# Zero-padded keys for the second attention score product, and mLSTM state products issued by head pairs

## The chip, the cores and the metric

The kernel runs on one core of one Trainium2 chip. The metric is the device time of one execution in microseconds (us); lower is better. Five engines work side by side, each through its own queue in order: TensorE (PE: matmuls and transposes, with its weight loads shown apart as PEld), VectorE (DVE), ScalarE (ACT), GpSimd (POOL) and SyncE (SP, which here only issues DMAs).

## What is computed

A trunk of two encoder layers is applied to 768 tokens of width 1024: a sample of 256 tokens and a prompt of 512, which share the weights but not the attention. All of it is in fp32. Cut to the mixer, in which the change lies, the reference is:

```python
def block(args):                       # differential attention, 4 heads, 2 components of 64 each
    s = jnp.einsum('bqhcd,bshcd->bhcqs', qi, k)
    p = jax.nn.softmax(s + bias[None, :, None], axis=-1)
    a = p[:, :, 0] - lam * p[:, :, 1]
    return jnp.einsum('bhqs,bshd->bqhd', a, v)
...
# bidirectional mLSTM, 4 heads, chunks of 128 positions; C_prev is the state at the chunk's border
sqk = jnp.einsum('bhcjd,bhcsd->bhcjs', qf, kc) * P
num = (e_inter[..., None] * jnp.einsum('bhcjd,bhcde->bhcje', qf, C_prev)
       + jnp.einsum('bhcjs,bhcse->bhcje', sqk, vc))
den = e_inter * jnp.einsum('bhcjd,bhcd->bhcj', qf, n_prev) + jnp.sum(sqk, -1)
h = num / jnp.maximum(jnp.abs(den), jnp.exp(-m_out))[..., None]
```

Both are joined, projected, normalised, and followed by a conv-gated feed-forward part with a second normalisation.

## The kernel before

Each layer runs in stages: gates and input projections of the mLSTM; four attention heads (`att_in(h)` projects a head's queries and keys, `att(h)` computes it), woven with the mLSTM and with projections that are needed later; the output projection with the first normalisation; the feed-forward part. In the profiled execution the attention heads and the mLSTM outputs stand at about 110 to 356 us (layer 0) and 1040 to 1292 us (layer 1).

Precision is kept by splitting fp32 numbers into two fp32r parts and taking three products. For the attention scores the two parts of the queries (64 rows each) are stacked over the 128 rows of the array: `sQ[:, c]` holds high and low part of component c's queries, `sK[:, c]` the high part of its keys twice. One product over 128 rows (line 701) so gives two of the three terms. The third, high query times the keys' low part `kL`, is a product over 64 rows (line 702): rows 0 to 63 for component 0, rows 64 to 127 for component 1. There are 96 of these pairs (2 layers, 4 heads, 6 query tiles, 2 components), 64 with 512 keys and 32 with 256. They write the two banks of PSUM with tag "s"; DVE reduces them (line 703), ACT exponentiates (707), DVE combines the components (708 to 710), PE transposes (713), ACT or DVE copies (715), PE multiplies with the values (717), ACT squares (719).

For the mLSTM outputs of a chunk (`lstm_out`), each head adds, for each direction, a state product over 64 rows (line 611; heads 0 and 2 lie on rows 0 to 63, heads 1 and 3 on rows 64 to 127) and an own-key product over 128 rows (612). Heads take the banks "L" and "t" in turn. DVE and ACT then empty the bank (614 to 619), ACT squares into a scratch tile `jk` (621). The decay factors `pt` of a chunk come by DMA into one of two buffers (568) and get a mask on DVE (570) and eight exponentials on ACT (572).

Products over 64 rows are also the scores of the mLSTM (596), and the state updates (551) use 64 columns of the array at a time. All other products use the whole array.

A scheduler fixes the order of each engine's queue when the kernel is built. `weave` mixes the generators in proportion to their steps, and `prio` shifts their priority; waiting is left to semaphores. An instruction that waits holds up all that stands behind it on its engine.

```python
PE.matmul(ps[:, :n], sQ[:, c, qtok], sK[:, c, keys], start=True, stop=False)
PE.matmul(ps[:, :n], sQ[r, c, qtok], kL[r, keys], start=False, stop=True)
```

Of the kernel before, what the change touches and what calls it, by code (L numbers as in the profile page):

```python
# [13 lines left out]
F32 = mybir.dt.float32  # L14
F32R = mybir.dt.float32r
AF = mybir.ActivationFunctionType
ALU = mybir.AluOpType
# [12 lines left out]
# tokens are held as [sample 256 | prompt 512]  # L30
# [65 lines left out]
class Weights:  # L96
    """Weight blocks of up to 528 columns in the order of their use, each split into two fp32r parts.
    A block is a piece of DRAM, or a difference of two earlier ones (a dict, for Strassen's products)."""

    def __init__(self, nc, raw_pool, hl_pool, prio):  # L100
        self.nc, self.raw_pool, self.hl_pool, self.prio = nc, raw_pool, hl_pool, prio
        self.dram, self.blocks = [], []     # DRAM pieces; (source, n, destination or None)
        self.uses, self.raw, self.hl = {}, {}, {}
        self.n_dma = self.n_conv = self.n_got = self.n_done = 0
        self.diff_pool = None
        self.urgency = PR_CONV

# [17 lines left out]
    def _pieces(self, src):  # L125
        """DRAM pieces that the conversion of a block reads"""
        if not isinstance(src, dict):
            return [src]
        if src.get("planned"):
            return []  # L130
        src["planned"] = True
        return self._pieces(src["a"]) + self._pieces(src["b"])

# [1 line left out]
    def _load(self):  # L135
        # slots are reused in turn
# [40 lines left out]
    def pump(self):  # L177
        # activations (with a destination of their own) take no slot
# [27 lines left out]
def trunk(ctx, nc, tc, d, o, depth=DEPTH):  # L206
# [13 lines left out]
    def prio(offset):  # L220
        """instructions that the scheduler takes as if written that many earlier (or later)"""
# [9 lines left out]
    def lam_products(v):  # L231
        # lam = exp(q1.k1) - exp(q2.k2) + lam_init, held negated
        v = v.rearrange("p (l a b) -> p l a b", l=DEPTH, a=4)
        V.tensor_tensor(out=lprod, in0=v[:, :, 0::2, :], in1=v[:, :, 1::2, :], op=ALU.mult)

# [9 lines left out]
    # two token tiles at once while the first weights arrive  # L245
# [19 lines left out]
    for l in range(depth):  # L265
# [19 lines left out]
        for kind, i in ffn_seq:  # L285
            if kind == "f":
                # Strassen-Winograd: B = [[g0, u0], [g1, u1]], halves of the rows of w_gate and w_up
# [26 lines left out]
    lprod = sm.tile([128, DEPTH, 2, 64], F32, tag="lprod", name="lprod", bufs=1)  # L314
# [11 lines left out]
    def late_constants():  # L326
        nc.scalar.dma_start(attg, d["attg"])
        nc.scalar.dma_start(convw, d["conv"])
        V.reduce_sum(lsum, lprod, axis=X)
# [12 lines left out]
    def tok_major(t, blocks, ps, cols):  # L342
        """ps[tok, :] = sum over k of x[tok, k] W[k, cols]"""
# [4 lines left out]
    def feat_major(blocks, psA, psB):  # L348
        """ps[feature, tok] = sum over k of W[k, feature] x[tok, k]"""
# [9 lines left out]
    def transposed_split(src, name, tag, hi, lo):  # L359
        """src [128, 512] -> four transposed 128x128 blocks, split into hi and lo [128, 4, 128]"""  # L360
# [7 lines left out]
    # =====================================================================================  # L368
    for l in range(depth):
        RA = ExitStack()  # L370
        ra = RA.enter_context(tc.tile_pool(name=f"ra{l}", bufs=1, reuse_waits="tile", side="right"))
        hq = ra.tile([128, NT, 512], F32, name="hq")         # mLSTM q | k, then h in their place
        av = ra.tile([128, NT, 512], F32, name="av")         # attention values, then the heads' transposed outputs
        sQ = ra.tile([128, 2, T], F32R, name="sQ")
        sK = ra.tile([128, 2, T], F32R, name="sK")
        kL = ra.tile([128, T], F32R, name="kL")
# [5 lines left out]
        cols = lp.tile([128, NT, 3, 8], F32, name="cols")   # w, exp(-m_out), e_end  # L382
# [10 lines left out]
        G.tensor_scalar(lstmg, lstmg, 0.5 * math.sqrt(128.0), 0.0, op0=ALU.mult, op1=ALU.add)   # rsl lacks the root  # L393
# [32 lines left out]
        def gates():  # L426
            GP = ExitStack()
            gp = GP.enter_context(tc.tile_pool(name=f"gp{l}", bufs=1, reuse_waits="tile"))
            rmask = gp.tile([128, 384], F32, name="rmask")
# [4 lines left out]
            for di in range(2):  # L434
                for pr in range(2):
                    for hh in range(2):
# [6 lines left out]
            V.tensor_scalar(g1, f, 0.0, 1.0, op0=ALU.min, op1=ALU.mult)               # min(f, 0)  # L443
            V.tensor_scalar(g2, f, 0.0, 1.0, op0=ALU.max, op1=ALU.mult)
            V.tensor_tensor(out=g1, in0=g1, in1=g2, op=ALU.subtract)                  # -|f|
            S.activation(g1, g1, AF.Exp)                                              # e
            V.tensor_scalar(g2, g1, 1.0, 1.0, op0=ALU.add, op1=ALU.mult)              # u = 1 + e
# [5 lines left out]
                                   in1=g1.rearrange("p a b c -> p (a b c)"), op0=ALU.add, op1=ALU.subtract)   # (u - 1) - e  # L453
            V.reciprocal(g2, g2)
            V.tensor_tensor(out=g1, in0=g1, in1=g2, op=ALU.mult)
            V.tensor_tensor(out=g3, in0=g3, in1=g1, op=ALU.subtract)                  # log1p(e)
# [7 lines left out]
            t1 = gp.tile([128, T], F32, name="t1")  # L464
# [22 lines left out]
            # stabiliser at the start of each chunk, in scan order  # L487
# [8 lines left out]
            V.tensor_tensor(out=mr, in0=mo, in1=bc, op=ALU.subtract)                  # M  # L496
# [4 lines left out]
            V.tensor_tensor(out=t1[0:64, :], in0=ig, in1=bc, op=ALU.subtract)         # w  # L501
# [83 lines left out]
        def lstm_out(lc, c):  # L585
# [5 lines left out]
            # heads on different rows of the array write different banks  # L591
# [11 lines left out]
            yield  # L603
            for h in range(4):
                pr, r = h // 2, slice((h % 2) * 64, (h % 2) * 64 + 64)
                pn = P(TAG_NUM[h], f"num{c}{h}")
                for di in range(2):
                    w = pn[:, di * 256:di * 256 + 129]
                    first = di not in dirs
                    if not first:  # L610
                        PE.matmul(w, qet[r, di, pr, :], cst[di, c][r, pr, :], start=True, stop=False)
                    PE.matmul(w, pt[:, di, h, :], vaug[:, c, h, :], start=first, stop=True)
# [7 lines left out]
                jk = lc.tile([128, 128], F32, tag="jk", name=f"jk{c}{h}", bufs=2)  # L620
                S.activation(jk, hs, AF.Square, accum_out=ssq[:, c, h:h + 1])
# [19 lines left out]
        def ev_lo(t, p):  # L641
# [6 lines left out]
            # 2 sigmoid(x) = exp(min(x, 0)) (1 + tanh(|x| / 2)), exact for either sign; the gain holds the half  # L648
# [9 lines left out]
        def att_in(h):  # L658
# [4 lines left out]
            for ui, uu in ((0, uq), (1, uk)):  # L663
# [4 lines left out]
                for ps, tk in ((pBu, slice(0, SB)), (pA, slice(SB, T))):  # L668
# [5 lines left out]
                    else:  # L674
# [4 lines left out]
                        V.tensor_tensor(out=kL[lo_, tk], in0=ps[lo_], in1=sK[lo_, 0, tk].bitcast(F32), op=ALU.subtract)  # L679
                        V.tensor_tensor(out=kL[hi_, tk], in0=ps[hi_], in1=sK[hi_, 1, tk].bitcast(F32), op=ALU.subtract)  # L680
                yield

# [1 line left out]
        def att(h):  # L684
            slope = 2.0 ** (-8.0 * (h + 1) / 4)
            for s0, s1 in SEQ_ORDER[h]:
# [6 lines left out]
                for qt in range(nq):  # L693
# [4 lines left out]
                    for c in range(2):  # L698
                        ps = P("s", f"s{h}{s0}{qt}{c}")
                        r = slice(c * 64, (c + 1) * 64)  # L700
                        PE.matmul(ps[:, :n], sQ[:, c, qtok], sK[:, c, keys], start=True, stop=False)
                        PE.matmul(ps[:, :n], sQ[r, c, qtok], kL[r, keys], start=False, stop=True)
                        V.tensor_tensor_reduce(out=tp[:, c, :n], in0=ps[:, :n], in1=dneg[:, 384 - 128 * qt:384 - 128 * qt + n], scale=-slope, scalar=3e38,
                                               op0=ALU.add, op1=ALU.min, accum_out=mn[:, c:c + 1])
                    # tp holds -scores: exp(min - tp) = exp(scores - max)
# [12 lines left out]
                    jk = ra.tile([128, 128], F32, tag="jk", name=f"jka{h}{s0}{qt}", bufs=1)  # L718
# [373 lines left out]
```

## Time and profile before

| | |
|---|---|
| device time, median of 3 runs | 1888.2 us (1887.25 to 1888.33) |
| span of the profiled execution (first to last instruction) | 1882.1 us |
| PE busy | 1838.9 us (98%) |
| DVE busy | 1342.5 us (71%) |
| ACT busy | 771.7 us (41%) |
| POOL busy | 238.8 us (13%) |
| granted TensorE clock, mean | 0.996 |

The page gives the profiled execution by its span alone, 6.1 us under the median of the runs. Busy shares are averages over stages with different limits. A PE that counts as busy is not one that works at its best rate: the profile's matmuls overlap in the pipeline, so what one of them costs is read from the time between its start and the next one's start, not from its own duration.

### The profile page before, as it was taken

How to read it: one execution, taken by the hardware profiler on the slowest of the kernel's cores; microseconds unless marked ns; L12 is line 12 of the kernel's file. 1: busy time of each engine (PE TensorE's matmuls, PEld its weight loads, DVE VectorE, ACT ScalarE, POOL GpSimd, SP SyncE). 2: the span in 40 equal slices, each digit the busy share in tenths (PEclk: the TensorE clock that was granted, in tenths of full speed). 3: DMA queues.
4: the chain of work that ended last, by engine and by line, in shares of the span. 5: the costliest groups of instructions: out<-in, count | busy, mean ns of one | idle time of the engine just before them, and what ended most of it. 6: DMA issues, size and time to landing. Idle time of an engine off the chain costs nothing. (4 is left out here: it accounts for less than half of the span.)

```text
span 1882.1 us, 26221 instructions
## 1 busy us (share of the span) xinstructions
PE 1838.9 (98%) x9692; PEld 1592.7 (85%) x9692; DVE 1342.5 (71%) x2576; ACT 771.7 (41%) x1624; POOL 238.8 (13%) x256
## 2 busy tenths in 40 slices
PE   8899999999999999999998999999999999999998
PEld 8777777779899899899897777777898998998996
DVE  5445776489886786787954457765898877877878
ACT  4344565334443343343332445654253432433330
POOL 1000101042110111110110011010411111111102
PEclk9999999999999999999999999999999999999999
DMA  6212110311222121122233021104022221221221
GB/s 196 85 49 68 46 45 23 135 40 62 85 81 66 59 82 62 64 77 87 100 107 90 18 68 51 40 23 150 25 68 96 68 79 62 71 76 57 79 62 67
DMA packets 83279, 134.94 MB, mean 72 GB/s; under 512 B 7984, under 2 KB 27056, under 8 KB 83152
## 3 DMA queue, kind: packets, MB, share of 16 engines
q1 hardware_dynamic: 82432, 132.90, 22.0%
q8 instruction: 76, 1.25, 0.3%
q14 instruction: 51, 0.42, 0.1%
q10 hardware_dynamic: 720, 0.37, 0.1%
HBM read 126.86 MB, written 6.39 MB: 71 GB/s over the span
## 5 line engine op out<-in xcount | busy, mean ns | idle before, releaser
L915 PE MATMUL p<-actA,wh 128*128 128x384 f32 x1408 | 363.4, 338 | 3.2 <-DVE g L940 3.2
L171 ACT ACTIVATE wh<-raw 128x512 fp32r<-128x512 f32 (+1 forms) x348 | 215.7, 629 | 299.8 <-PE p L915 109.7
L172 DVE TENSOR_TENSOR wl<-raw,wh 128x512 fp32r<-128x512 f32 (+1 forms) x348 | 242.7, 707 | 95.9 <-ACT wh L171 95.4
L915 PE MATMUL p<-actB,wh 128*128 128x384 f32 x1056 | 270.1, 337 | 0.0
L915 PEld LDWEIGHTS p<-actA,wh 128*128 128x128 f32 x1408 | 254.7, 188 | 5.8 <-DVE g L940 3.8
L915 PE MATMUL p<-actA,wl 128*128 128x384 f32 x704 | 237.3, 337 | 0.0
L149 POOL TENSOR_TENSOR T<-raw,raw 128x512 f32<-128x512 f32 x88 | 120.7, 1374 | 836.5 <-DVE wl L172 483.6
L975 PE MATMUL dn<-wh,actB 128*128 128x512 f32 x576 | 208.7, 396 | 1.1 <-DVE acc L982 1.1
L171 ACT ACTIVATE wh<-T 128x512 fp32r<-128x512 f32 x176 | 108.3, 628 | 220.2 <-DVE acc L982 105.0
L915 PEld LDWEIGHTS p<-actB,wh 128*128 128x128 f32 x1056 | 191.2, 188 | 0.0
L975 PE MATMUL dn<-wh,ring 128*128 128x512 f32 x480 | 179.2, 397 | 1.8 <-DVE acc L982 1.8
L915 PE MATMUL p<-actB,wl 128*128 128x384 f32 x528 | 177.2, 336 | 0.0
L982 DVE TENSOR_TENSOR acc<-acc,dn 128x512 f32<-128x512 f32 x144 | 98.1, 681 | 72.0 <-PE dn L975 71.8
L172 DVE TENSOR_TENSOR wl<-T,wh 128x512 fp32r<-128x512 f32 x176 | 129.6, 748 | 22.1 <-ACT wh L171 21.9
L975 PEld LDWEIGHTS dn<-wh,actB 128*128 128x128 f32 x576 | 108.0, 188 | 28.7 <-DVE acc L982 2.8
L915 PEld LDWEIGHTS p<-actA,wl 128*128 128x128 f32 x704 | 132.2, 188 | 0.1
L871 PE MATMUL wo<-wh,actB 128*128 128x512 f32 x384 | 122.7, 396 | 0.0
L975 PE MATMUL dn<-wl,actB 128*128 128x512 f32 x288 | 113.2, 393 | 0.0
L975 PEld LDWEIGHTS dn<-wh,ring 128*128 128x128 f32 x480 | 90.0, 188 | 24.8 <-DVE acc L982 4.4
L915 PEld LDWEIGHTS p<-actB,wl 128*128 128x128 f32 x528 | 99.1, 188 | 0.0
L356 PE MATMUL aqkA<-actA,wh 128*128 128x512 f32 x256 | 97.7, 407 | 0.0
L975 PE MATMUL dn<-wl,ring 128*128 128x512 f32 x240 | 94.6, 394 | 0.0
(263 smaller groups left out, 3442.8 us busy)
## 6 DMA issues: line engine op xcount, KB each, us to landing
raw<-in_w_g_dram SPq DMA_DIRECT2D x88, 256.0 KB, 2.7
raw<-in_w_u_dram SPq DMA_DIRECT2D x88, 256.0 KB, 2.7
raw<-in_w_down_dram SPq DMA_DIRECT2D x88, 256.0 KB, 2.9
raw<-in_w_out_dram SPq DMA_DIRECT2D x32, 256.0 KB, 2.6
pt<-scr_m SPq DMA_DIRECT2D x12, 512.0 KB, 5.9
raw<-in_w_c_dram SPq DMA_DIRECT2D x16, 264.0 KB, 3.9
raw<-in_w_av_dram SPq DMA_DIRECT2D x16, 256.0 KB, 4.8
raw<-in_w_aq_dram SPq DMA_DIRECT2D x16, 256.0 KB, 3.5
```

What stands on the lines that cost most here:

```text
L149: src["engine"].tensor_tensor(out=src["tile"], in0=a, in1=b, op=ALU.subtract)
L171: self.nc.scalar.activation(h, v, AF.Identity)
L172: self.nc.vector.tensor_tensor(out=l, in0=v, in1=h.bitcast(F32), op=ALU.subtract)
L356: PE.matmul(psA, w, actA[:, k, b, SB:T], start=n == 0, stop=n == 23)
L871: PE.matmul(p, actB[:, k, a, t * 128:(t + 1) * 128], units[k][1 + b], start=n + i == 0, stop=n == 7 and i == 2)
L915: PE.matmul(ps, blk[1 + a][:, k * 128:(k + 1) * 128], x[:, k, b, :], start=k + i == 0, stop=k == 3 and i == 2)
L975: PE.matmul(p, x, (wh_, wl_)[b], start=k + i == 0, stop=k == nf - 1 and i == 2)
L982: V.tensor_tensor(out=z, in0=z, in1=p, op=ALU.add)
```

## The change

- `kL` becomes two planes of 128 rows. Plane 0 holds component 0's low keys on rows 0 to 63 and zeros below, plane 1 component 1's on rows 64 to 127 and zeros above. The zeros are written by two memsets on POOL once per layer. The second score product then runs over all 128 rows, with the same stationary operand as the first.
- The state products of a pair of heads, of all their directions, are issued first, then the own-key products of both heads. Both banks of the pair are asked for together.
- To make room, the squares go where a dead value lies: the mLSTM's into `pt` instead of `jk`, the attention's into `aT` instead of another `jk`; the gates' mask shares the tile `t1`; the lambda products are formed in place, and their sum is taken at once.

```diff
-        kL = ra.tile([128, T], F32R, name="kL")
+        kL = ra.tile([128, 2, T], F32R, name="kL")
+        G.memset(kL[64:128, 0].bitcast(F32), 0.0)
+        G.memset(kL[0:64, 1].bitcast(F32), 0.0)
...
-                        V.tensor_tensor(out=kL[lo_, tk], in0=ps[lo_], in1=sK[lo_, 0, tk].bitcast(F32), op=ALU.subtract)
-                        V.tensor_tensor(out=kL[hi_, tk], in0=ps[hi_], in1=sK[hi_, 1, tk].bitcast(F32), op=ALU.subtract)
+                        V.tensor_tensor(out=kL[lo_, 0, tk], in0=ps[lo_], in1=sK[lo_, 0, tk].bitcast(F32), op=ALU.subtract)
+                        V.tensor_tensor(out=kL[hi_, 1, tk], in0=ps[hi_], in1=sK[hi_, 1, tk].bitcast(F32), op=ALU.subtract)
...
-                        PE.matmul(ps[:, :n], sQ[r, c, qtok], kL[r, keys], start=False, stop=True)
+                        PE.matmul(ps[:, :n], sQ[:, c, qtok], kL[:, c, keys], start=False, stop=True)
...
+            pns = {}
             for h in range(4):
-                pr, r = h // 2, slice((h % 2) * 64, (h % 2) * 64 + 64)
-                pn = P(TAG_NUM[h], f"num{c}{h}")
-                for di in range(2):
-                    w = pn[:, di * 256:di * 256 + 129]
-                    first = di not in dirs
-                    if not first:
-                        PE.matmul(w, qet[r, di, pr, :], cst[di, c][r, pr, :], start=True, stop=False)
-                    PE.matmul(w, pt[:, di, h, :], vaug[:, c, h, :], start=first, stop=True)
+                if h % 2 == 0:
+                    pair = [(hh, P(TAG_NUM[hh], f"num{c}{hh}")) for hh in (h, h + 1)]
+                    for di in dirs:
+                        for hh, pn in pair:
+                            r = slice((hh % 2) * 64, (hh % 2) * 64 + 64)
+                            PE.matmul(pn[:, di * 256:di * 256 + 129], qet[r, di, hh // 2, :], cst[di, c][r, hh // 2, :],
+                                      start=di == dirs[0], stop=False, skip_group_check=True)
+                    for hh, pn in pair:
+                        for di in range(2):
+                            PE.matmul(pn[:, di * 256:di * 256 + 129], pt[:, di, hh, :], vaug[:, c, hh, :],
+                                      start=not dirs and di == 0, stop=di == 1, skip_group_check=True)
+                    pns.update(pair)
+                pn = pns.pop(h)
...
-                jk = lc.tile([128, 128], F32, tag="jk", name=f"jk{c}{h}", bufs=2)
-                S.activation(jk, hs, AF.Square, accum_out=ssq[:, c, h:h + 1])
+                S.activation(pt[:, 0, h, :], hs, AF.Square, accum_out=ssq[:, c, h:h + 1])
...
-                    jk = ra.tile([128, 128], F32, tag="jk", name=f"jka{h}{s0}{qt}", bufs=1)
-                    S.activation(jk, pu[:, qt * 128:(qt + 1) * 128], AF.Square, accum_out=ssu[:, qt:qt + 1])
+                    S.activation(aT[:, 0:128], pu[:, qt * 128:(qt + 1) * 128], AF.Square, accum_out=ssu[:, qt:qt + 1])
```

In the built order of PE, a run is an unbroken stretch of products that use a part of the array (64 rows, or 64 columns), between products that use all of it. The change alters their number:

| runs, by the product that opens them | before | changed |
|---|---|---|
| second score product (L702; L709 in the changed kernel) | 96 | 0 |
| mLSTM state products (L611; L614) | 62 | 44 |
| mLSTM scores (L596; L598) | 20 | 24 |
| state updates (L551; L553) | 12 | 16 |
| one small product of the gates (L515; L517) | 2 | 2 |
| all | 192 | 86 |

PE, chunk 3 of layer 0, heads 2 and 3: `num` is a head's bank, `cst` the state and `vaug`, `pt` the operands of the own-key product, `lo` a projection. Before:

```order
L611 MATMUL num_2476<-cst_1670,qet_2117 128x129
L612 MATMUL num_2476<-vaug,pt_2105 128x129
L611 MATMUL num_2476<-cst_1751,qet_2117 128x129
L612 MATMUL num_2476<-vaug,pt_2105 128x129
L730 MATMUL aoT_2546<-ident,ao_2544 128x128 x2
L346 MATMUL lo_2723<-wh_1561,actA 128x512
L346 MATMUL lo_2723<-wl_1562,actA 128x512
L611 MATMUL num_2489<-cst_1670,qet_2117 128x129
L612 MATMUL num_2489<-vaug,pt_2105 128x129
L611 MATMUL num_2489<-cst_1751,qet_2117 128x129
L612 MATMUL num_2489<-vaug,pt_2105 128x129
```

The same place on PE in the changed kernel, with a head's second score product (L709) now a product of 128 rows:

```order
L709 MATMUL s_2661<-kL,sQ 128x512
L614 MATMUL num_2448<-cst_1664,qet_2097 128x129
L614 MATMUL num_2448<-cst_1743,qet_2097 128x129
L618 MATMUL num_2448<-vaug,pt_2085 128x129 x2
L736 MATMUL aoT_2516<-ident,ao_2514 128x128 x2
L345 MATMUL lo_2686<-wl_1634,actA 128x512
L708 MATMUL s_2665<-sK,sQ 128x512
L614 MATMUL num_2449<-cst_1664,qet_2097 128x129
L614 MATMUL num_2449<-cst_1743,qet_2097 128x129
L618 MATMUL num_2449<-vaug,pt_2085 128x129 x2
L709 MATMUL s_2665<-kL,sQ 128x512
```

Each head's two directions now stand side by side, one run in place of two, but the scheduler has kept the two heads of the pair apart.

DVE, the mask of chunk 4's decay factors in layer 0 (`pt` with `tri`), among the chunk before's work: `kq` are the mLSTM scores, `sg` the output gate, `tp` and `mn` the attention's reduction. Before:

```order
L598 TENSOR_TENSOR pt_2105<-kq_2416,pt_2105 128x4x128
L628 SCALAR_TENSOR_TENSOR hq<-hq,rsl,lstmg 128x128 x4
L570 TENSOR_TENSOR pt_2394<-pt_2394,tri 128x512 x2
L598 TENSOR_TENSOR pt_2105<-kq_2420,pt_2105 128x4x128
L715 COPY aT_2444<-aT_2441 128x256
L654 SCALAR_TENSOR_TENSOR sg_2527<-sgt_2528,sg_2527 128x512
L722 SCALAR_TENSOR_TENSOR sm_2368<-sm_2368 128x2
L703 ISA tp_2553,mn_2554<-s_2556,dneg 128x512
```

The same place on DVE in the changed kernel:

```order
L710 ISA tp_2523,mn_2524<-s_2526,dneg 128x512
L710 ISA mn_2524 128x1
L636 SCALAR_TENSOR_TENSOR hq<-hq,rsl,lstmg 128x128 x4
L600 TENSOR_TENSOR pt_2085<-kq_2391,pt_2085 128x4x128
L717 SCALAR_TENSOR_TENSOR tp_2400<-tp_2400,cc_2402 128x256
L662 SCALAR_TENSOR_TENSOR sg_2497<-sgt_2498,sg_2497 128x512
L600 TENSOR_TENSOR pt_2085<-kq_2395,pt_2085 128x4x128
L572 TENSOR_TENSOR pt_2369<-pt_2369,tri 128x512 x2
L722 COPY aT_2419<-aT_2416 128x256
```

The mask (now L572) stands behind the second score multiplication, the gate and an attention reduction that it stood ahead of. In the feed-forward parts no engine's order differs; at the start of layer 0 some projections of the first two token tiles change places on PE, and POOL has the two memsets among its first constants.

## Rows read from the trace of the kernel before

**Rows 1.** The page's first part: busy us, share of the span, instructions.

```profile
PE 1838.9 (98%) x9692; PEld 1592.7 (85%) x9692; DVE 1342.5 (71%) x2576; ACT 771.7 (41%) x1624; POOL 238.8 (13%) x256
```

**Rows 2.** Windows by stage: stretch, its length, busy us (count) by engine, clock, DMA.

```profile
110.00:160.00 50.00, 49.86 (x228) 36.42 (x226) 23.49 (x63) 21.86 (x58) 0.83 (x2) 1.00 0.06 18
236.00:310.00 74.00, 73.73 (x390) 54.98 (x388) 50.56 (x167) 45.20 (x142) 8.50 (x12) 1.00 0.13 36
```

**Rows 3.** Waits of PE in the whole span: us, times, longest.

```profile
PE s L701 <- ACT sK L677: 1.2, 2, 0.6
```

**Rows 4.** Timeline of PE, layer 0, head 1: start us, us, line, tiles.

```profile
202.34 0.50 PE L701 MATMUL s<-sK,sQ 128*128 128x512 f32 x1
202.77 0.50 PE L702 MATMUL s<-kL,sQ 64*128 64x512 f32 x1
203.20 0.50 PE L701 MATMUL s<-sK,sQ 128*128 128x512 f32 x1
203.63 0.50 PE L702 MATMUL s<-kL,sQ 64*128 64x512 f32 x1
204.06 0.50 PE L356 MATMUL aqkA<-actA,wh 128*128 128x512 f32 x1
204.40 0.60 PE L713 MATMUL aT<-ident,tp 128*128 128x128 f32 x4
```

**Rows 5.** Timeline of PE, layer 0, head 0.

```profile
112.93 0.38 PE L702 MATMUL s<-kL,sQ 64*128 64x256 f32 x1
113.23 0.50 PE L346 MATMUL lv<-wh,actA 128*128 128x512 f32 x1
113.57 0.40 PE L346 MATMUL lv<-wl,actA 128*128 128x512 f32 x1
113.80 0.63 PE L346 MATMUL lv<-wh,actA 128*128 128x512 f32 x2
```

**Rows 6.** Timeline of PEld (weight loads); in brackets idle time before, and what ended it.

```profile
113.34 0.19 PEld L346 LDWEIGHTS lv<-wl,actA 128*128 128x128 f32 x1
...
202.77 0.18 PEld L702 LDWEIGHTS s<-kL,sQ 64*128 64x128 f32 x1 [0.25 <-issue]
```

**Rows 7.** Timeline of PE, layer 0, an mLSTM output of chunk 0.

```profile
199.71 0.39 PE L612 MATMUL num<-vaug,pt 128*128 128x129 f32 x2
200.02 0.49 PE L611 MATMUL num<-cst,qet 64*128 64x129 f32 x2
200.44 0.49 PE L612 MATMUL num<-vaug,pt 128*128 128x129 f32 x2
200.76 0.50 PE L717 MATMUL u<-av,aT 128*128 128x128 f32 x3
```

**Rows 8.** Timelines of DVE and PE, layer 0, chunk 3: emptying a bank, its next use.

```profile
258.63 0.16 DVE L614 SCALAR_TENSOR_TENSOR den<-num,cols 128x2 f32<-128x2 f32 x1 [1.53 <-PE num L612]
...
261.04 0.35 DVE L619 SCALAR_TENSOR_TENSOR hq<-num,den,hq 128x128 f32<-128x128 f32 x1
...
261.98 0.49 PE L702 MATMUL s<-kL,sQ 64*128 64x512 f32 x1
261.98 0.49 PE L611 MATMUL num<-cst,qet 64*128 64x129 f32 x2
```

**Rows 9.** Timelines of DVE and PE, layer 0, head 0.

```profile
129.07 0.75 DVE L710 SCALAR_TENSOR_TENSOR tp<-tp,cc 128x512 f32<-128x512 f32 x1
...
130.27 0.60 PE L713 MATMUL aT<-ident,tp 128*128 128x128 f32 x4
...
131.63 1.07 PE L717 MATMUL u<-av,aT 128*128 128x128 f32 x8
132.45 0.48 PE L346 MATMUL lv<-wh,actA 128*128 128x512 f32 x1
```

**Rows 10.** Timelines of SP, ACT and DVE, layer 0, the decay factors of chunk 4.

```profile
247.75 0.55 SPq L568 DMA_DIRECT2D pt<-scr_m  x1
...
250.75 0.30 ACT L621 ACTIVATE jk<-hq 128x128 f32<-128x128 f32 x1
...
253.60 1.28 DVE L570 TENSOR_TENSOR pt<-pt,tri 128x512 f32<-128x512 f32 x2
```

**Rows 11.** Timeline of POOL at the start of layer 1.

```profile
943.81 0.74 POOL L450 MEMSET gs<- 128x768 f32 x1
...
1012.05 1.19 POOL L546 TENSOR_TENSOR ke<-hq,cols 128x256 f32<-128x256 f32 x2 [57.78 <-ACT cols L529]
```

More of the change, by code (lines that the diff above doesn't have):

```diff
@@ L233, in lam_products @@
         v = v.rearrange("p (l a b) -> p l a b", l=DEPTH, a=4)
-        V.tensor_tensor(out=lprod, in0=v[:, :, 0::2, :], in1=v[:, :, 1::2, :], op=ALU.mult)
+        V.tensor_tensor(out=v[:, :, 0::2, :], in0=v[:, :, 0::2, :], in1=v[:, :, 1::2, :], op=ALU.mult)
+        V.reduce_sum(lsum, v[:, :, 0::2, :], axis=X)
     W = Weights(nc, wr, wh, prio)
@@ L313, in trunk @@
     S.activation(warm, mhalf[:, 0:1], AF.Identity)
-    lprod = sm.tile([128, DEPTH, 2, 64], F32, tag="lprod", name="lprod", bufs=1)
     lsum = sm.tile([128, DEPTH, 2], F32, tag="lsum", name="lsum", bufs=1)
@@ L328, in late_constants @@
         nc.scalar.dma_start(convw, d["conv"])
-        V.reduce_sum(lsum, lprod, axis=X)
         S.activation(lsum, lsum, AF.Exp)
@@ L428, in gates @@
             gp = GP.enter_context(tc.tile_pool(name=f"gp{l}", bufs=1, reuse_waits="tile"))
-            rmask = gp.tile([128, 384], F32, name="rmask")
+            t1 = gp.tile([128, T], F32, name="t1")
+            rmask = t1[:, 0:384]
             G.memset(rmask, 1.0)
@@ L463, in gates @@
             bc = gp.tile([64, T], F32, name="bc")
-            t1 = gp.tile([128, T], F32, name="t1")
             t2 = gp.tile([128, T], F32, name="t2")
@@ L699, in att @@
                         ps = P("s", f"s{h}{s0}{qt}{c}")
-                        r = slice(c * 64, (c + 1) * 64)
                         PE.matmul(ps[:, :n], sQ[:, c, qtok], sK[:, c, keys], start=True, stop=False)
-                        PE.matmul(ps[:, :n], sQ[r, c, qtok], kL[r, keys], start=False, stop=True)
+                        PE.matmul(ps[:, :n], sQ[:, c, qtok], kL[:, c, keys], start=False, stop=True)
                         V.tensor_tensor_reduce(out=tp[:, c, :n], in0=ps[:, :n], in1=dneg[:, 384 - 128 * qt:384 - 128 * qt + n], scale=-slope, scalar=3e38,
```

## Prediction

> **What bounds the kernel now.** I read the page's first part, then the windows by stage, PE's waits, and last the timeline of PE around the products that change. PE counts as busy for 98% of the span [rows 1], and in the stages of attention and mLSTM it has hardly an idle moment: 49.9 of 50 us with head 0, 73.7 of 74 with head 2, at the full clock of 2.4 GHz (granted 1.00). DVE has 50.6 of those 74 us to do, ACT 45.2 [rows 2]. In the whole span PE waits 1.2 us for operands of the scores [rows 3]. So PE sets the pace of these stages, and time taken from PE is time gained until another engine's work, or a wait, comes to stand in its place.
>
> A busy PE can still lose time, and the starts of its matmuls show where. Two products with 512 columns that use the whole array start 0.23 us apart (113.57 to 113.80 [rows 5]). The four score products of a query tile start 0.43 us apart, and the matmul that follows them takes 0.34 [rows 4]. Where the array goes from 128 rows to 64, the weight load of the 64-row product stands idle for 0.25 us, although nothing that the profile shows holds it up [rows 6]. A stretch of products on part of the array, a run, so costs time at its entry and its exit.
>
> **The price of one run.** From 202.34 to 204.40 five matmuls of 512 columns take 2.06 us; at 0.23 to 0.235 they would take 1.18. The excess is 0.88, but about 0.10 of it is the exit of a run just before (0.10 is what a matmul behind a run is slow by: 113.23 to 113.57 is 0.34 [rows 5]). That leaves 0.78 for two runs, 0.39 each. The state products give the same: a product of 129 columns in fp32 is two matmuls at 0.10 to 0.11 us (131.63 to 132.45 is 0.82 for eight of the same kind [rows 9]). From 199.71 to 200.76 stand six of them, which would take 0.64 and take 1.05, an excess of 0.41 for one run [rows 7]. I take 0.39.
>
> **The change, part by part.**
>
> *Padded keys.* Of 96 second score products, each a run of its own, none is left: 96 x 0.39 = 37.4 us less on PE. The matmul itself gets no longer, since it streams the same columns, and its weights are as many columns as before.
>
> On the weights there is a rule to weigh. A load on all 128 rows (0.19 us) starts at 113.34, while the 128-row matmul that started at 113.23 is running, and the next matmul starts at 113.57, in step [rows 5, 6]: the load is hidden. The Trainium skill (TensorE: Matmul & The Clock Gate, Part 3, The mechanism) says that a weight load overlaps with running matmuls only when it goes to other row groups. By that rule the padded product, which uses every row group as its predecessor does, could hide no load. This trace contradicts it for 128-row products, so the sum goes by the row.
>
> *State products by pairs.* The order of the changed kernel brings the heads' directions together but leaves the heads of a pair mostly apart. Runs that a state product opens go from 62 to 44: 18 x 0.39 = 7.0 us less. The mLSTM scores and the state updates, which partly stood in a run with a second score product, open 8 runs more: 3.1 us back. Products on different halves of the rows can run at the same time (a score product and a state product both start at 261.98 [rows 8]), but only four times in the new order do the states of two heads stand next to each other; at two matmuls of 0.11 that is under 1 us, and I take nothing.
>
> Together PE loses 192 - 86 = 106 runs: 106 x 0.39 = 41.3 us. With the 0.41 of the state run for all, it would be 43.5. With only what shows at the product itself and its follower (0.43 less 0.23, and 0.10), the price is 0.30 and the sum 31.8; I keep 0.39, since whole stretches, neighbours included, come to it [rows 4, 7].
>
> *Zeros.* Two memsets of 64 x 768 per layer. One of 128 x 768 takes 0.74 us, and POOL in layer 1 is then idle for 57.8 us [rows 11]; POOL is busy 13% of the span [rows 1]. Nothing. Were that cover gone, it would be under 3 us in all.
>
> *Squares into `pt` and `aT`.* The work is the same. But the DMA of a chunk's decay factors, which could start when the last own-key product had read the buffer, now waits for the last square: it was issued at 247.75, and the square begins at 250.75 and takes 0.30, so 3.3 us later. SP, which waits with it, has only weights behind it. The mask on DVE, at 253.60 [rows 10], is late next. In the new order it stands behind a second score multiplication, a gate and a reduction, about 0.7 us each, some 2.1 us of work. So DVE may stand still for about 1.2 us, four times a layer, 10 us in all. Below, none of it reaches PE, since DVE has 23 us free in such a stage of 74 [rows 2]; above, all of it. As PE has projections between the steps, I take 3 us.
>
> *Head 0.* The path from the first component's scores to the transposes is work of DVE and ACT. The transposes start at 130.27, the result that they read is there at 129.82 [rows 9]: 0.45 us of slack. PE now comes there sooner by the second component's runs, 0.5 us. The difference and a semaphore, some 0.1 us, become a wait in 12 tiles: 1.5 us.
>
> *Banks of the states.* A bank is asked for from 258.63 and empty at 261.39; its next head begins at 261.98 [rows 8], 0.59 of slack. PE has two runs less in between, 0.8 us, but the new order puts more projections there. I take 0.2 us for eight such places: 1.5 us.
>
> *The in-place lambda products, the shared mask tile:* as many instructions on the same engine, nothing.
>
> **Sum.** 41.3 - 3 - 1.5 - 1.5 = 35 us. Against the profiled span of 1882.1 that gives 1847. The runs shown have a median of 1888.2, 6.1 over that span, and I put the same on top: **1853 us**, a ratio of 0.981. The bounds: no new wait and the higher price give 1888.2 - 43.5 = 1845. The lower price with the waits as taken gives 1888.2 - 31.8 + 6 = 1862; the price as taken with all 10 us of DVE's waits and twice the others gives 1888.2 - 41.3 + 16 = 1863; both at once, 1872, of which I take half the way, 1868.
>
> **The rivals.**
>
> 1. *DVE and ACT take over.* In heads 1 to 3 the queues of DVE, ACT and PE pass banks back and forth. If the loop through DVE sets the pace as soon as PE is some us faster, half the gain stays there: 15 to 20 us in all, 1868 to 1873. For it: DVE with 50.6 of 74 us [rows 2], and slack of only 0.45 and 0.59 us [rows 8, 9]. Against it: PE would need 69 us there, so DVE stays at 73%, and DVE's own waits in this stage are mostly for PE (1.53 us before 258.63 [rows 8]).
>
> 2. *The padded load is exposed.* If a load could not run under a matmul on the same rows, each padded product would take 0.19 more: 96 x 0.19 = 18 us, so 1871. That is the rule above. Against it stands every pair of rows of plain projections [rows 5, 6].
>
> 3. *The pair holds both banks: slower.* State products of both heads need both banks empty, and behind them in PE's queue stand the own-key products. If PE stood still at each of the 24 pairs until the second bank is empty, that costs up to the 2.76 us from 258.63 to 261.39 [rows 8]: 66 us, less the gain of 41.3, so 1913. It decides from 41.3 / 24 = 1.7 us of wait per pair. For it: "t" also serves the attention's transposes. Against it: the built order has 44 runs and not 24, so the second head's states are put later where its bank is late.
>
> 4. *No new wait at all:* 1845 to 1847.
>
> That the change does not do what it says holds only for the pairing, and that is in the sum: 24 runs in place of 44 would be 7.8 us more.
>
> **How the numbers follow.** The forecast has 0.72, rival 1 0.14, rival 2 0.03, rival 3 0.04, rival 4 0.07. A measurement of this kernel can tell about 0.2%, 3.8 us, from no change. The forecast, rivals 2 and 4 and nearly all of rival 1 are faster by more: 0.95. For no change I leave 0.01 of rival 1, and 0.04 is slower. The range from 1845 to 1868 holds the forecast with its bounds, rival 4 and the edge of rival 1, over 8 in 10.
>
> **What would show it.** Right: the four score products start 0.23 to 0.24 us apart; the weight load of the second has no idle time before it; PE's busy time and the span both fall by 33 to 41 us, the heads' stages alone being shorter, and the feed-forward parts as long as before. Own-key products start in pairs behind one run. The step on waits is wrong if PE's waits in the heads' stages come to over 15 us or to under 2, and the mask on DVE shows a wait for the DMA of `pt` if that step is right. If the score products stay 0.4 us apart, the price of a run was misread, and with it the forecast.

## The result, and the profile after

The changed kernel takes 1855.74 us (median of 4 runs, 1854.93 to 1856.37); the kernel before, beside it, 1887.84 (4 runs, 1887.25 to 1888.33). The ratio is 0.983, with a 95% interval of 0.982 to 0.985: faster by 32.1 us. The forecast was 1853 us, in a range of 1845 to 1868.

The first part of the page after, to be held against [rows 1]: PE is busy 34.6 us less, its weight loads 5.6 us less, and the other engines are as long as before to within some 3 us.

```profile
PE 1804.3 (97%) x9692; PEld 1587.1 (86%) x9692; DVE 1340.4 (72%) x2576; ACT 768.9 (41%) x1624; POOL 241.9 (13%) x260
```

Windows of the kernel before: the four heads of layer 0, each from its first score product to the next head's (the last one to the first product of the output projection), then all four of layer 1. Columns as in [rows 2].

```profile
111.00:180.30 69.30, 69.28 (x354) 53.11 (x354) 31.00 (x75) 28.36 (x70) 4.08 (x5) 1.00 0.15 46
180.30:240.70 60.40, 60.40 (x350) 45.95 (x350) 43.70 (x134) 34.89 (x106) 6.14 (x10) 1.00 0.15 45
240.70:313.90 73.20, 72.37 (x383) 53.98 (x382) 50.43 (x165) 44.40 (x138) 8.50 (x12) 1.00 0.13 37
313.90:347.10 33.20, 32.60 (x159) 23.12 (x160) 24.39 (x65) 23.13 (x59) 1.44 (x1) 1.00 0.10 33
1046.30:1282.30 236.00, 234.57 (x1245) 176.08 (x1246) 149.65 (x438) 130.82 (x373) 20.13 (x27) 1.00 0.14 41
```

The same stages of the changed kernel:

```profile
115.60:181.80 66.20, 65.94 (x355) 52.74 (x355) 30.50 (x75) 28.05 (x71) 4.16 (x5) 1.00 0.15 49
181.80:237.70 55.90, 55.49 (x345) 44.33 (x346) 41.73 (x130) 31.18 (x96) 6.66 (x10) 1.00 0.15 44
237.70:305.70 68.00, 66.33 (x388) 52.58 (x387) 51.72 (x170) 47.03 (x149) 9.02 (x12) 1.00 0.14 44
305.70:334.50 28.80, 28.25 (x160) 23.01 (x161) 24.17 (x65) 23.07 (x60) 1.42 (x1) 1.00 0.11 36
1034.90:1253.60 218.70, 215.86 (x1244) 172.55 (x1245) 148.06 (x438) 129.26 (x372) 21.24 (x27) 1.00 0.15 44
```

The heads go from 236.1 to 218.9 us in layer 0 and from 236.0 to 218.7 in layer 1: 34.5 us. PE's idle time in them (length less busy time) doubles, from 1.43 to 2.84 us in layer 1, and stays small; the clock is full in both. The rest of each layer, the feed-forward part above all, is as long as before (594.8 us in layer 0 in both). Yet the spans differ only by 28.4 us (1882.1 and 1853.7). What is missing lies ahead of the heads: their first score product starts at 111.0 us before and at 115.6 after.

The timeline of PE answers to [rows 4]: the score products now start 0.22 to 0.24 us apart, where they started 0.43 apart. (The first, 0.34, follows the state updates, a run.)

```profile
199.84 1.06 PE L724 MATMUL u<-av,aT 128*128 128x128 f32 x8
200.82 0.66 PE L553 MATMUL cu<-vaug,ke 128*64 128x129 f32 x8
201.41 0.50 PE L708 MATMUL s<-sK,sQ 128*128 128x512 f32 x1
201.75 0.40 PE L709 MATMUL s<-kL,sQ 128*128 128x512 f32 x1
201.99 0.39 PE L708 MATMUL s<-sK,sQ 128*128 128x512 f32 x1
202.21 0.39 PE L709 MATMUL s<-kL,sQ 128*128 128x512 f32 x1
202.45 0.40 PE L355 MATMUL aqkA<-actA,wh 128*128 128x512 f32 x1
```

The weight loads of the same place, to be held against [rows 6]: the 0.25 us of idle time before the second product's load is gone, and each load of 0.19 us starts while the product ahead of it runs.

```profile
201.52 0.19 PEld L709 LDWEIGHTS s<-kL,sQ 128*128 128x128 f32 x1
201.75 0.19 PEld L708 LDWEIGHTS s<-sK,sQ 128*128 128x128 f32 x1
201.99 0.19 PEld L709 LDWEIGHTS s<-kL,sQ 128*128 128x128 f32 x1
```

To see what the runs cost in the two traces, I took every matmul at the border of a run, the time from its start to the next start, less the usual spacing of its shape (0.23 us for 512 columns, 0.11 to 0.13 for 128 and 129). "Given back" is what the stage did not get shorter by, although the excess is gone. For layer 0:

| | head 0 | head 1 | head 2 | head 3 | sum |
|---|---|---|---|---|---|
| runs, before and after | 15, 3 | 29, 19 | 39, 20 | 12, 0 | 95, 42 |
| excess, before and after (us) | 5.2, 0.5 | 10.8, 7.1 | 14.9, 8.1 | 4.8, 0.0 | 35.6, 15.7 |
| excess gone (us) | 4.7 | 3.7 | 6.8 | 4.8 | 20.0 |
| stage shorter by (us) | 3.1 | 4.5 | 5.2 | 4.4 | 17.2 |
| given back (us) | 1.6 | -0.8 | 1.6 | 0.4 | 2.8 |

In the whole kernel the excess falls from 72.0 us at 192 runs (0.375 each) to 32.6 at 86 (0.379 each): 39.4 us gone, some 5 of them given back in the heads.

Not every run costs that much. The eight state updates at 200.82 in the timeline above, products on 64 columns of the array, take 0.59 us until the next start, 0.07 us each, where eight products that use all of it took 0.82 ([rows 9], 131.63 to 132.45). With the eight products ahead of them and the product behind, 199.84 to 201.75, they take 1.91 us; at 0.11 and 0.23 us each it would be 1.99. What such a run loses at its borders it wins back inside. Runs of second score products, state products and mLSTM scores cost 0.38 to 0.40 us each; the 12 runs that state updates open before, and 16 after, cost about nothing. Counted over whole runs, inner products included, the excess falls from some 70 to some 29 us.

**The transposes of head 0.** Before, the last matmul ahead of the transposes of [rows 9]:

```profile
130.03 0.39 PE L346 MATMUL lv<-wl,actA 128*128 128x512 f32 x1
```

The same place in the changed kernel, DVE's result and then PE:

```profile
132.49 0.75 DVE L717 SCALAR_TENSOR_TENSOR tp<-tp,cc 128x512 f32<-128x512 f32 x1
...
133.03 0.40 PE L345 MATMUL lv<-wl,actA 128*128 128x512 f32 x1
133.39 0.63 PE L720 MATMUL aT<-ident,tp 128*128 128x128 f32 x4
```

Before, the transposes start 0.24 us after that matmul, the usual spacing, and 0.45 us after the result is there. After, they start 0.36 us behind the matmul and 0.15 behind the result (133.24): now they wait for it. All six tiles of layer 0 show the same: 0.23 to 0.24 us before, 0.29 to 0.60 after, 0.9 us more in all, and 0.8 in layer 1. Little of it counts as idle, since the record of the matmul ahead lasts 0.4 us.

**Ahead of the heads.** ACT before, at the end of the gates: a table load of 1.28 us, done long before the exponential that waits for DVE.

```profile
58.36 1.28 ACT L507 ACT_TABLE_LOAD   x1
64.11 0.84 ACT L507 ACTIVATE t<-t 64x768 f32<-64x768 f32 x1 [4.47 <-DVE t L506]
65.16 0.21 ACT L512 ACTIVATE ae<-ae 64x6 f32<-64x6 f32 x1 [0.20 <-DVE ae L511]
```

ACT after: the load itself now waits, and the exponential comes behind it.

```profile
64.59 1.28 ACT L509 ACT_TABLE_LOAD   x1 [5.82 <-DVE t L508]
65.89 0.84 ACT L509 ACTIVATE t<-t 64x768 f32<-64x768 f32 x1
66.75 0.21 ACT L514 ACTIVATE ae<-ae 64x6 f32<-64x6 f32 x1
```

PE waits for `ae` at the gates' small product, 4.09 us before and 5.26 after, in each layer. The cause stands in the built order, first before, then after:

```
L507 ACT_TABLE_LOAD
L507 ACTIVATE t_683<-t_683 64x768 [waits DVE_49]
...
L509 EVENT_SEMAPHORE [waits DVE_49]
L509 ACT_TABLE_LOAD
L509 ACTIVATE t_633<-t_633 64x768 [waits Pool_49]
```

With the mask in `t1`, POOL's memset writes all 128 rows of the tile whose rows 64 to 127 the exponential overwrites. So it waits for two engines. It carries the wait for POOL itself; the wait for DVE, the late one, is an instruction of its own, which stands ahead of the table load too.

**The decay factors.** SP, ACT and DVE after, to be held against [rows 10]: the DMA is issued when the last square of the chunk has ended, as the prediction had it, but the mask on DVE follows in a row of work and waits for nothing.

```profile
248.11 0.30 ACT L629 ACTIVATE pt<-hq 128x128 f32<-128x128 f32 x1
...
248.52 0.38 SPq L570 DMA_DIRECT2D pt<-scr_m  x1
...
252.55 0.68 DVE L600 TENSOR_TENSOR pt<-kq,pt 128x512 f32<-128x512 f32 x1
253.15 1.28 DVE L572 TENSOR_TENSOR pt<-pt,tri 128x512 f32<-128x512 f32 x2
```

### The profile page after: what moved, and what is told of

It reads as the page before. It is cut to its first block, busy times and chain, and to the rows that moved or that the text cites. A ratio compares the mean times of both kernels' runs of the same rounds, so it can differ in the third digit from the quotient of the medians.

```text
span 1853.7 us, 26256 instructions
## 1 busy us (share of the span) xinstructions
PE 1804.3 (97%) x9692; PEld 1587.1 (86%) x9692; DVE 1340.4 (72%) x2576; ACT 768.9 (41%) x1624; POOL 241.9 (13%) x260
## 4 chain that ended last, share of the span: by engine, by line
PE 78%; DVE 13%; ACT 5%; issue 2%; POOL 2%; DMA 1%; SPq 0%; DVEq 0%; ACTq 0%; POOLq 0%
PE p L921 32%; PE dn L981 16%; PE wo L877 5%; PE aqkA L355 3%; PE lv L345 3%; PE lo L345 3%; PE aqkB L354 2%; DVE wl L172 2%; PE c1a L345 2%; PE u L724 2%; PE av L345 2%; PE c1b L345 2%; PE num L618 1%; ACT wh L171 1%; PE num L614 1%
```

## The experiments

**The theory.** The gain is the number of runs times their price, and what the heads give back is small; the edits that make room cost something that the prediction put at nothing, above all the table load. **The rivals:** the loss ahead of the heads is the clock or chance and the edits are free; or banks and order, not the number of runs, decide. A median below is that of the runs of one kernel, with their extremes; the kernel before beside them had 1887.8, 1887.1, 1887.2 and 1887.4 us in the four groups.

**The mask on half of the tile.** The changed kernel, with one edit:

```diff
-            G.memset(rmask, 1.0)
-            G.memset(rmask[:, ::128], 0.0)
+            G.memset(rmask[0:64], 1.0)
+            G.memset(rmask[0:64, ::128], 0.0)
```

> The changed kernel, but the gates' mask is set on rows 0 to 63 alone, the only rows that the scans read, so that the exponential on rows 64 to 127 no longer waits for POOL besides DVE. Theory A (the shared tile's second wait put the load of ACT's function table behind the wait for DVE, 1.28 us in each layer, and PE's longer stall there kept the clock at 1.2 GHz for longer): about 1850 us, 5 to 6 us under the changed kernel's 1855.7, with the table load again ahead of the wait and layer 0's first score product near 111 us of the span, not 115.6. Theory B (the 5.8 us that the start of the layers lost come from the two zero memsets or the changed order at the start): 1855 to 1856, first score product still near 115.

Measured: 1853.21 us (1851.17 to 1853.81), ratio 0.981 (0.980 to 0.983), 2.5 us under the changed kernel. ACT has its load ahead of the wait again:

```profile
59.21 1.28 ACT L509 ACT_TABLE_LOAD   x1
64.97 0.84 ACT L509 ACTIVATE t<-t 64x768 f32<-64x768 f32 x1 [4.48 <-DVE t L508]
```

PE's wait is 4.12 us, the heads are unchanged (218.8 us each). So the mechanism is shown, at 1.2 us a layer. The time lies between the two theories: layer 0's first score product starts at 114.1 us, not near 111, so the rest of the late start did not come back. What it is, the next run tells.

**The kernel before once more**, unchanged, for its spread:

> The kernel before, unchanged, profiled once more. The profile shown of before had a span of 1882.1 us at a mean clock of 0.996. If that execution was one of the faster ones, because PE's stretches at 1.2 GHz after its stalls were short in it, another has stretches of 6.8 us where that one had 3.4, a span near 1885.8 at 0.993 to 0.994, and the same heads' stages of 236 us per layer. If that execution was an ordinary one, the span is 1882 again and the 3 us that the changed kernel's starts lost beside the table load belong to the change.

Measured: 1887.34 us, ratio 1.000 (0.999 to 1.001). Its profiled execution has a span of 1886.9 us, against the 1882.1 of the one that the prediction was made from. The heads are as long (236.2 and 236.1), but their first score product starts at 115.1 us, not 111.0. Windows of the first execution, around PE's wait at the gates' small product (the last three columns are the granted clock, the DMA share and GB/s):

```profile
60.00:70.00 10.00, 5.91 (x24) 4.42 (x23) 5.18 (x14) 1.05 (x2) 0.00 (x0) 0.83 0.02 6
70.00:80.00 10.00, 10.00 (x49) 8.27 (x48) 0.00 (x0) 1.49 (x5) 1.19 (x2) 0.99 0.00 0
```

The same windows of the second execution of the same kernel:

```profile
60.00:70.00 10.00, 5.88 (x22) 4.77 (x22) 5.86 (x14) 1.34 (x3) 0.00 (x0) 0.74 0.03 6
70.00:80.00 10.00, 10.00 (x46) 8.07 (x45) 0.00 (x0) 1.45 (x5) 1.19 (x2) 0.92 0.00 0
```

After the same wait of 4.1 us the clock is back at 2.4 GHz later in the second one: 0.92 in the mean from 70 to 80 us, and PE issues 46 matmuls there and not 49. So of the 5.8 us by which the starts of the two layers differ between the profiles of before and after, 2.3 are the table load, and the rest is the execution that the first profile happened to show. Held against this second execution, the changed kernel's two starts are later by 1.5 us together, and those of the kernel with the small mask are together as early.

**The edits for room alone**: the kernel before with the squares in `pt` and `aT`, the mask in `t1` and the lambda products in place.

> The kernel before with only the edits that make room: squares into pt and aT, the shared mask tile, the lambda products in place. 64-row second score products and the old order of the state products stay. It has 196 runs where the kernel before has 192. Theory A (the edits cost what the start of the layers lost): 1893 to 1895 us. Theory B (the edits are free, as the prediction had it): 1887 to 1890 us.

Measured: 1895.72 us (1894.67 to 1896.94), ratio 1.004 (1.003 to 1.005): slower by 7.9 us. The waits on the small product are 5.3 us each again (2.3 of it), and the heads are 2.2 us longer each, of which four more runs are 1.5 in all. A second kernel takes back two of the edits:

```diff
-            G.memset(rmask, 1.0)
-            G.memset(rmask[:, ::128], 0.0)
+            G.memset(rmask[0:64], 1.0)
+            G.memset(rmask[0:64, ::128], 0.0)
...
-                S.activation(pt[:, 0, h, :], hs, AF.Square, accum_out=ssq[:, c, h:h + 1])
+                jk = lc.tile([128, 256], F32, tag="ke", name=f"jk{c}{h}", bufs=2)[:, 0:128]
+                S.activation(jk, hs, AF.Square, accum_out=ssq[:, c, h:h + 1])
```

> The kernel before with the edits that make room (side_only, 1895.7 us), less two of them: the mask memset on rows 0 to 63, and the mLSTM squares in the slots of ke, not in pt. 192 runs, as in the kernel before. Theory A (the 7.9 us of side_only are the table load behind its wait, 2.4, and the squares in pt with the four runs that they add, 5 to 6): time 1887 to 1888.5, heads' stages 236.2 each, aB waits 4.1. Theory B (the attention's squares in aT cost it): heads' stages 237.5 to 238.5 each, time 1891 to 1893.

Measured: 1888.11 us (1884.91 to 1888.93), ratio 1.000 (0.999 to 1.001), heads of 236.2 us. So the mask on the whole tile and the squares in `pt` are the 7.9 us; the squares in `aT` and the products in place cost nothing. In the old order of the state products, the squares in `pt` cost some 5 us: what is left of the 7.9 without the table load, not a run of its own. How they cost it stays open; with the edits alone, too, DVE's masks wait for the DMA only ahead of the heads (8.4 us in two waits).

**Padding alone** (state products in the old order) **and pairing alone** (64-row keys), both with all edits for room:

> The changed kernel with the old order of the state products: padded keys and the edits that make room. 106 runs against the changed kernel's 86. Theory A (a run costs about 0.37 us wherever it stands): 1855.7 + 20 x 0.37 = 1863 us. Theory B (the pairing gains little because its bank waits give it back): 1855 to 1857 us.

> The changed kernel with 64-row second score products as before: the pairing and the edits that make room. 174 runs against 192 before. Theory A: 18 x 0.37 = 6.7 us gained, about 5.8 us lost at the starts of the layers, 1886 to 1888 us. Theory B (pairing helps more than its runs say, because states on different rows run at the same time): 1880 us or less.

Measured: padding alone 1865.43 us (1863.56 to 1866.77), ratio 0.988 (0.987 to 0.989), with 106 runs; pairing alone 1885.08 (1883.64 to 1886.56), ratio 0.999 (0.998 to 1.000), with 174 runs. With the edits alone (196 runs) and the whole change (86) this makes a square, in which each part is added with and without the other:

| from | to | runs fewer | us less | per run |
|---|---|---|---|---|
| edits alone | padding alone | 90 | 30.3 | 0.34 |
| pairing alone | the whole change | 88 | 29.3 | 0.33 |
| edits alone | pairing alone | 22 | 10.6 | 0.48 |
| padding alone | the whole change | 20 | 9.7 | 0.48 |

The parts add up: -7.9 + 30.3 + 9.7 = 32.1 us. Padding brings less than its runs by the count, pairing more. Part of the surplus of pairing lies outside the heads' stages. These, 238.4 and 238.3 us with the edits alone, are 222.7 and 222.7 with padding alone, 233.5 and 233.3 with pairing alone and 218.9 and 218.7 with both. In them padding gains 31.3 and 29.2 us, 0.35 and 0.33 a run, and pairing 9.9 and 7.8, 0.45 and 0.39 a run. Pairing alone just about pays for the edits that make room.

**Is it the squares in `pt`, in the changed kernel?** Two tries to free the DMA from the squares, both with the small mask: squares in the dead tile `ke`, as in the second diff above, and squares in `qkt`:

```diff
-                S.activation(pt[:, 0, h, :], hs, AF.Square, accum_out=ssq[:, c, h:h + 1])
+                S.activation(qkt[:, h, :], hs, AF.Square, accum_out=ssq[:, c, h:h + 1])
```

> The mask memset on rows 0 to 63 as in mask64 (1853.2 us), and the mLSTM squares in a scratch of their own (slots of the tile ke, which is dead by then), so that the DMA of the decay factors pt no longer waits for the last square. 86 runs as before. Theory A (the squares in pt delay the DMA, DVE's mask and with them PE): the heads' stages shorten by about 1.5 us each, from 218.8 to 217.3, and the time is near 1850. Theory B (the delay is hidden, since DVE has time to spare): heads' stages within 0.5 us of 218.8, time 1852 to 1854. In both the mask on DVE (L572) shows no wait for the DMA of pt.

> The kernel with the mask on 64 rows (1853.2 us), but the mLSTM's squares go into the dead transposed queries and keys of the chunk instead of the decay factors, so that the DMA of the next decay factors waits for PE alone, as before the change. Theory A (the later DMA holds up DVE's queue and with it PE, some 1.5 us a layer): 1850 us. Theory B (PE has other work there, the delay is hidden): 1853 us, heads' stages of 218.8 us as before.

Measured: in `ke` 1855.58 us (1854.48 to 1856.80), ratio 0.983 (0.982 to 0.984), heads of 219.8 and 219.9; in `qkt` 1860.38 (1859.82 to 1861.03), ratio 0.986 (0.984 to 0.987), heads of 223.5 and 221.5. Both have 86 runs, and neither is faster than the 1853.2 us with the squares in `pt`. So no gain from an earlier DMA shows in the changed kernel. Neither try is a clean test, since each brings waits of its own, behind which a small gain could hide: in the second the next copy into `qkt` waits for the squares, and the first one moves the order too. PE's waits with the squares in `ke`:

```profile
PE s L709 <- ACT sK L686: 3.2, 2, 1.6
...
PE kq L598 <- DVE qkt L583: 2.5, 4, 0.8
```

With the squares in `pt` the first of these is 1.8 us, and in place of the second stands one of 0.9 for `pt`.

**Other banks, fewer runs.** The table of banks decides which products can stand together. The bank of the mLSTM scores drawn from L and t in turn:

```diff
-TAG_KQ = "LL"
+TAG_KQ = "Lt"
```

> As squares_in_qkt, but the mLSTM scores of the odd heads go to bank t instead of L, so that the two products of a chunk can follow each other. 84 runs, 2 less. Theory A (runs set the price): about 1 us under squares_in_qkt. Theory B (bank t is wanted by the attention's transposes, and waits come in): 2 us or more above it.

> mask64_ke with the banks of the mLSTM scores drawn from L and t in turn instead of L alone; 84 runs against 86. Theory A (runs decide): two runs less are 0.7 us, time 0.5 to 1.5 us under mask64_ke. Theory B (the banks decide): the bank t, which serves the attention's transposes too, brings waits of PE for it, and the time is 2 us or more above mask64_ke.

> mask64 (1853.2 us) with the banks of the mLSTM scores drawn from L and t in turn instead of L alone; 80 runs against 86, four of them fewer at the state products. Theory A (runs decide): six runs less at 0.38 us are 2.3 us, time 1850 to 1852. Theory B (the bank t, which serves the attention's transposes too, brings waits of PE and of DVE, as in kq_lt_ke): the time is 1856 us or more, with PE's wait for DVE's sQ or for tp longer than in mask64 (6.3 and 0.2 us).

Measured: on the squares in `qkt` 1859.00 us (1856.41 to 1859.94; 84 runs for 86), 1.4 less, with ranges that touch; on the squares in `ke` 1860.91 (1860.14 to 1861.79; 84 for 86), 5.3 more; on the small mask 1852.84 (1850.90 to 1855.41; 80 for 86), which can't be told from its 1853.21. In the last, PE's waits for `sQ` and `sK` have grown by 0.7 and 1.2 us (to 7.0 and 3.0), nearly as much as six runs are worth (2.3). The three don't agree, and neither theory holds for all. Last, the mLSTM outputs of heads 1 and 3 on a bank that serves the projections (d), with head 2 on t:

```diff
-TAG_NUM = "LtLt"
+TAG_NUM = "Ldtd"
```

> As squares_in_qkt, but the four heads' mLSTM outputs take banks L, d, t, d instead of L, t, L, t, so that a bank need not be emptied before the next pair's states. 76 runs, 10 less. Theory A (runs at 0.37 to 0.48 us): 4 to 5 us under squares_in_qkt. Theory B (the projections lose one of their three d banks at these places and wait for their evacuation): no gain, or a loss.

Measured, on the squares in `qkt`: 1880.82 us (1877.44 to 1886.70), ratio 0.997 (0.996 to 0.998). Ten runs fewer, and 20.4 us more. PE's waits:

```profile
PE aqkB L354 <- DVE sQ L681: 9.9, 4, 3.2
...
PE aoT L736 <- DVE ao L732: 4.9, 6, 1.5
PE u L724 <- ACT aT L722: 4.3, 6, 0.7
```

The profiled execution is the slowest of its eleven, 1886.70 us. A window of it in layer 1, in which the granted clock is 0.73 in the mean, between the levels of 1.2 and 2.4 GHz:

```profile
1110.00:1135.00 25.00, 23.87 (x119) 17.55 (x117) 14.10 (x44) 10.29 (x29) 2.15 (x4) 0.73 0.08 22
```

The three waits come to 19.1 us; with the old banks the first two were 5.5 and 3.3, and PE's waits at the third line 0.4 in all. The clock, too, is lower in the heads' stages, in which the changed kernel had 1.00. How much each of the two costs was not taken apart.

**The best kernel** is the changed one with the mask on half of the tile, at 1853.2 us (1852.8 with the other banks for the scores, which is the same).

## Why the prediction was right, and where it was off

- *What bounds it.* PE, in the heads' stages, at the full clock: right. Only these stages got shorter, by 34.5 us where the sum had 35.
- *The price of a run.* 0.39 us was read from two places; over all runs it is 0.375 to 0.379. The 106 runs so are 39.4 us and not 41.3. The sum took every run as equal; of the 8 that were to open anew, the four of the state updates cost nothing.
- *Padding and pairing.* Predicted 37.4 for the padding, less 3.1 for the runs that it leaves open, and 7.0 for the pairing. Taken apart, padding brought 29 to 30 us and pairing 10: the first was too high, the second too low, and that the two make the sum right is luck. By the starts a run costs the same in both, so the difference should be waits that come and go with the order, which is argued and not shown: one of them shows, PE's for `sK`, 2.8 us with padding alone and 1.8 after the whole change. The others were not named.
- *The zero on the shared mask tile* was the step that failed: "as many instructions on the same engine, nothing". It costs 2.3 to 2.5 us, by a wait that came to stand ahead of a table load. The instructions were counted and the waits were not; the changed order, read with its waits, shows it. Without it the forecast of 1853 is met to 0.2 us.
- *Zeros and lambda products: nothing.* Right for the products, as far as the kernel with the remaining edits shows it (1888.1 us against 1887.2 beside it); POOL has 3.1 us more to do.
- *The later DMA of `pt`.* Its mechanism is there (the DMA waits for the last square), but no mask in the heads' stages waits for it. The wait that has grown is ACT's for the mask, 2.97 us at 253.87 where it was 0.30, and ACT has 21 of 68 us free there. The 3 us taken for it are not seen in the changed kernel. In the old order the squares cost some 5 us, more than was taken, but not by a mask that waits. What stands next on SP is the next chunk's `qet`, at 262.12, and not weights.
- *Head 0.* Predicted 1.5 us for both layers in waits of the transposes; the count gives 1.6 a layer, 3.2. The wait is there, and of the size that was forecast, 0.9 and 0.8 us; it does not show in PE's idle time, which is only 0.2 to 0.3 us longer there. How the rest of the 3.2 is lost stays open.
- *Banks of the states.* 1.5 predicted; in heads 1 to 3 together 1.2 a layer is given back, 2.4 in all, but the rows don't say by which bank. All waits together were put at 6 us and come to some 5.
- *"6.1 over that span".* The offset was no constant. A run's time lies 1.8 us over the span of the same execution (1855.45 and 1853.7); the other 4 us were the profiled execution, which was faster than the median. The sum on top of the median was right, the reason given for it wasn't.
- *The rivals.* DVE and ACT didn't take over: DVE has 51.7 of 68 us to do in head 2 and PE stays at 98%. The exposed load, 18 us, isn't there: the load of a padded product starts under the product ahead of it, on the same rows. This contradicts the rule of the Trainium skill (TensorE: Matmul & The Clock Gate, Part 3, The mechanism) here too, 0.19 us of load within a spacing of 0.23. The same section also lets a load be pulled ahead when it goes to a background buffer for weights; that would agree, but no run here shows where the loads go. That a pair holds both banks cost nothing of the size of 66 us, since the order keeps most pairs apart; the run on other banks, 20.4 us slower by waits for banks and a lower clock, shows that such waits can be dear, though not this one.
- *The checks it named.* Spacing, load, PE's busy time (34.6) and PE's idle time in the heads (5.7 us, between 2 and 15) came out as said. The span fell by 28.4, below the 33 to 41, and the wait of the mask is missing.

## What to carry to other kernels

On a TensorE that is 98% busy, look for places where products on part of the array stand between products on all of it: here a stretch on 64 rows costs some 0.39 us, and multiplying by zeros, at the same number of columns, is cheaper than going in and out. Why it costs that was not taken apart, and the stretches on 64 columns, whose products follow each other faster, cost nothing. PE's idle time hides waits that are shorter than the overlap of its records; the spacing of the starts shows them. An edit that only makes room shares a buffer, and with it a wait: list what each instruction waits for before and after, and look at what the wait now holds up. Order and banks can cost more than the runs they save, so each part of such a change is worth timing on its own.

## What was not expected of the hardware

- A table load that stood ahead of a wait, hidden, came to stand behind it when the activation had a second engine to wait for, since the second wait became an instruction of its own: 1.28 us of load, 1.17 us more wait on PE in each layer. The Trainium skill (ScalarE: Activation LUTs, What ACT_TABLE_LOAD costs) gives 1283 ns for the load and a switch some 2.66 us in all; the load has that length here, but two exposed switches cost 2.5 us together, so the second part doesn't show.
- After the same wait of 4.1 us, the clock of the same kernel is back at its upper level sooner in one execution than in another (0.99 or 0.92 in the mean of the same 10 us). Runs of the kernel before spread from 1883.5 to 1890.1 us.

Not tried: padding the mLSTM's state products as well, and a scratch of the old size for the squares in the changed kernel.
